# Moving the sums for block products and the mixer's norm broadcast in a two-block network

## The chip, the cores and the metric

The kernel runs on one core of a Trainium2 chip. The metric is the device time of one execution in microseconds (us). The median of three runs before the change is 1705.44 (1704.96 to 1706.16). Engines: TensorE (PE, matmuls), VectorE (DVE), ScalarE (ACT), GpSimd (POOL), SyncE (SP, issues DMAs).

## The reference

The input x has 512 tokens of 1024 features, in float32. A first block of two layers (gated linear attention beside differential attention) is followed by a second block, cut here to what matters:

```python
def swiglu(h, w_in, w_out):
    gate, up = jnp.split(h @ w_in, 2, axis=-1)
    return (jax.nn.silu(gate) * up) @ w_out

def hybrid_mixer(h, w_in, ...):
    za, zb, zg = jnp.split(h @ w_in, [2 * A_WIDTH, 2 * A_WIDTH + 3 * B_WIDTH], axis=-1)
    u, v = jnp.split(jax.nn.gelu(za), 2, axis=-1)
    y_a = spatial_gating(u, v, sgu_norm, sgu_w, sgu_b) @ w_proj_a   # v is normed in it
    ...
    return merged @ w_out

x = x + 0.5 * swiglu(rmsnorm(x, ffn1_norm), ffn1_w_in, ffn1_w_out)
x = x + hybrid_mixer(rmsnorm(x, mix_norm), ...)
x = x + 0.5 * swiglu(rmsnorm(x, ffn2_norm), ffn2_w_in, ffn2_w_out)
return rmsnorm(x, final_norm)
```

## The kernel before

x stays on the chip as eight tiles `xs[k]` of 128 features x 512 tokens. Each float32 product is three fp32r matmuls (`mm3`, L174 to L176): both operands are split into a rounded part hi (ACT copies it) and a rest lo (DVE subtracts). So every tile of weights costs ACT and DVE work before PE can use it.

Large products are done as 2x2 block products with seven multiplications instead of eight (`block_jobs`, L367). A unit loads four raw weight tiles of 1 MB (a11, a21, a22, a12), and forms sums of them: one by an adding DMA on POOL's queue (L393), a21 + a22 (L399) and a21 - a11 (L405) on DVE, one more by an adding DMA (L409). `parts` (L376) splits such a sum into hi and lo; for a name in `turn`, lo is made by a negated ACT copy and an adding POOL DMA (L383, L384) instead of DVE. Seven steps of 24 matmuls follow, in three accumulators (tm): step 0 uses x itself (xgh, xgl), steps 1 and 2 use sums of x (bth, btl), step 3 other sums (bnh, bnl). A `hook` is called after each half step; in steps 0, 2 and 3 it copies an accumulator out of PSUM (fa at L1083 in the feed-forward, va at L1243 in the mixer), and only then can the next step write there.

The sums of x are made by `block_sums(p)` (L323 to L342) for each of four pairs of x tiles: ACT makes te, bth and bnh, DVE the sums tt and te (L330 to L333), btl (L165) and bnl (L340). `t4_parts` (L345) later splits another part of te into xg.

The feed-forward starts with two ordinary input jobs of two products each (`in_job`, hidden tiles fg, fu, fh), then come units of block products. In the first feed-forward each of these four products is followed by one block sum. The mixer starts with the unit v; three of its block sums are made as x is finished (`after`, L301), the fourth from the hook at the start of step 0. `norm` makes the roots of the mean square: narrow matmuls nps (L245), a power on POOL (rs, L229), and 2 us of estimated time later a broadcast by eight matmuls nbc (L256) and the copy rsb (L259).

What sets the order: the jobs are generators. `run` (L186) issues them along an estimated clock and puts in side work (`light`, such as `norm` with its two delays) once it is due; behind that, a scheduler with an estimated timeline sets each engine's final row. Each engine executes its row strictly in order, so an instruction that waits holds all that stands behind it.

Of the kernel before, what the change touches and what calls it, by code (L numbers as in the profile page):

```python
# [13 lines left out]
ALU = mybir.AluOpType  # L14
# [53 lines left out]
PAUSE = 5.0  # L68
TURN = 10.0
TURN0 = 1.5  # L70


@with_exitstack
def block_kernel(ctx: ExitStack, tc: tile.TileContext, a, out):
# [219 lines left out]
                k0 += 1  # L294
                yield 2.6 * n / S

    def residual(o, k, scale, nxt, sums=False):

        V.scalar_tensor_tensor(xs[k], o, scale, xs[k], op0=ALU.mult, op1=ALU.add)
        after(k, nxt, sums)  # L300

    def after(k, nxt, sums=False):
        if k == 0:
            for key in ("rs", "bc", "nrs", "nrs2"):
                st.pop(key, None)
            st["xg"], st["bt"], st["bn"], st["be"] = [], [], [], []
        sumsq(k)
        st["xg"].append(split(xs[k], "xg", scale=nxt(k)))
        if sums and k in (2, 4, 6):
            block_sums(k // 2 - 1, nxt)  # L310
        if k == KT - 1:
            light(norm(2.5, 2.0))

# [48 lines left out]
        A.activation(hi, x, AF.Copy, scale=g)  # L364
        V.scalar_tensor_tensor(lo, x, g, f(hi), op0=ALU.mult, op1=ALU.subtract)

    def block_jobs(src, hook, turn=()):  # L367


        q, banks = {}, {}  # L370

        def load(name, i):
            q[name] = wraw.tile([P, 2112], F32, tag="raw", name=nm("raw"))[:, 0:4 * S]
            nc.sync.dma_start(q[name], src[i])

        def parts(name):  # L376
            pieces = []
            for j in range(2):
                r = q[name][:, 2 * j * S:2 * j * S + 2 * S]
                hi, lo = (wsp.tile([P, 1024], F32R, tag=v, name=nm(v)) for v in ("hi", "lo"))  # L380
                A.activation(hi, r, AF.Copy)  # L381
                if name in turn:
                    A.activation(lo, r, AF.Copy, scale=-1.0)  # L383
                    nc.gpsimd.dma_start(lo, r, accum_op=ALU.add)  # L384
                else:
                    V.tensor_tensor(lo, r, f(hi), op=ALU.subtract)  # L386
                pieces.append(tuple(v.rearrange("p (k n) -> p k n", n=S) for v in (hi, lo)))
            return pieces

        def l1():  # L390
            load("a11", 0)
            load("a21", 2)
            nc.gpsimd.dma_start(q["a21"], q["a11"], accum_op=ALU.add)  # L393
            return parts("a11")

        def l2():
            load("a22", 3)
            ps = parts("a21")
            V.tensor_tensor(q["a21"], q["a21"], q["a22"], op=ALU.add)  # L399
            return ps  # L400

        def l3():
            load("a12", 1)
            ps = parts("a21")
            V.tensor_tensor(q["a11"], q["a21"], q["a11"], op=ALU.subtract)  # L405
            return ps

        def l4():
            nc.gpsimd.dma_start(q["a21"], q["a12"], accum_op=ALU.add)  # L409
            return parts("a11")  # L410


        steps = [
            (l1, "b11", "a", True), (l2, "t3", "b", True), (l3, "t2", "a", False), (l4, "t1", "a", False),
            (lambda: parts("a12"), "b21", "c", True), (lambda: parts("a22"), "t4", "b", False),
            (lambda: parts("a21"), "b22", "a", False),
        ]

        def step(i, name, chain, first):
            def body(ps):  # L420
                if first:
                    banks[chain] = [psum("tm") for _ in range(2)]
                hook(i, -1, banks)
                for t in range(2):
                    for p in range(4):
                        ah, al = block(name, p, t)
                        wh, wl = (v[:, p % 2] for v in ps[p // 2])
                        mm3(banks[chain][t], ah, al, wh, wl, first and p == 0, p == 3, True)
                        yield 0.68
                    hook(i, t, banks)  # L430
            return body

        return [(ld, None, step(i, *which)) for i, (ld, *which) in enumerate(steps)]


# [601 lines left out]
    def ffn_jobs(i, nxt):  # L1037
# [3 lines left out]
        def in_job(c):  # L1041
            def body(ps):
                xg = st["xg"]
                os = []
                for j in range(2):
                    o = psum("fm")
                    yield from fm1(o, [ps[j]], xg)
                    os.append(o)

                    if i == 0:  # L1050
                        block_sums(2 * c + j, gains)
                    elif c + j == 0:
                        block_sums(3, gains)
                yield from until("bc")
                g = slot("fg")
                V.tensor_tensor(g, os[0], st["bc"], op=ALU.mult)
                A.activation(g, g, AF.Silu)
                u = slot("fu")
                V.tensor_tensor(u, os[1], st["bc"], op=ALU.mult)
                V.tensor_tensor(g, g, u, op=ALU.mult)  # L1060
                hid.append(split(g, "fh"))
            return body
# [12 lines left out]
        def unit(n):  # L1075
            v, h = {}, {"more": n not in (0, 2, 4)}

            def hook(i, t, banks):
                if t < 0:
                    return  # L1080
                if i in (0, 2, 3):
                    v[i, t] = slot("fa")
                    A.activation(v[i, t], banks["a"][t], AF.Copy)  # L1083
                if i == 1 and n == 0 and t == 1:
                    for p in range(4):
                        t4_parts(p)
                if i == 3:
                    V.tensor_tensor(v[3, t], v[3, t], banks["b"][t], op=ALU.add)
                if i == 4:
                    V.tensor_tensor(v[0, t], v[0, t], banks["c"][t], op=ALU.add)  # L1090
                    A.activation(v[0, t], v[0, t], AF.Silu, scale=roots("rs", t))
                if i == 5:
                    V.tensor_tensor(v[2, t], v[2, t], banks["b"][t], op=ALU.add)
                    V.scalar_tensor_tensor(v[0, t], v[2, t], roots("nrs", t), v[0, t], op0=ALU.mult, op1=ALU.mult)
                    h[t] = v[0, t]
                if i == 6:
                    g = slot("fg")
                    A.activation(g, banks["a"][t], AF.Silu, scale=roots("rs", 2 + t))
                    V.scalar_tensor_tensor(g, v[3, t], roots("nrs", 2 + t), g, op0=ALU.mult, op1=ALU.mult)
                    h[2 + t] = g  # L1100
                    if t == 1:
                        light(turned(h), TURN if h["more"] else TURN0)

            return block_jobs(a[f"ffs{i}"][n], hook)

        def add_out(o, k, hf):
            if hf < 2:
                V.scalar_tensor_tensor(xs[k], o, 0.5, xs[k], op0=ALU.mult, op1=ALU.add)
            elif nxt is not None:
                residual(o, k, 0.5, nxt, True)  # L1110
            else:
                V.scalar_tensor_tensor(xs[k], o, 0.5, xs[k], op0=ALU.mult, op1=ALU.add)
                sumsq(k)
                gain(k)
# [94 lines left out]
    def mixer_jobs():  # L1209
# [16 lines left out]
        def v_unit():  # L1226
# [7 lines left out]
                gv[t, b] = g, ss  # L1234

            def hook(i, t, banks):
                if t < 0:
                    if i == 0:
                        block_sums(3, gains)
                    return  # L1240
                if i in (0, 2, 3):
                    v[i] = v.get(i, []) + [slot("va")]
                    A.activation(v[i][t], banks["a"][t], AF.Copy)  # L1243
# [17 lines left out]
                            A.activation(g, g, AF.Copy, scale=r)  # L1261
                        vs.append((g0, g1))

            return block_jobs(a["mv"], hook, ("a11",))

        def conv(n, h):

# [12 lines left out]
        def cx_unit(n):  # L1280
            v, h = {}, {}

            def hook(i, t, banks):
                if t < 0:
                    return
                if i in (0, 2, 3):
                    v[i, t] = slot("ca")
                    A.activation(v[i, t], banks["a"][t], AF.Copy)
                for at, chain, k in ((3, "b", 3), (4, "c", 0), (5, "b", 2)):
                    if i == at:  # L1290
                        V.tensor_tensor(v[k, t], v[k, t], banks[chain][t], op=ALU.add)
                if i == 5:
                    V.scalar_tensor_tensor(v[0, t], v[2, t], roots("nrs2", t), v[0, t], op0=ALU.mult, op1=ALU.mult)
                    h[t] = v[0, t]
                    if t == 1 and n == 1:
                        for p in range(4):
                            block_b12(p, gains)
                if i == 6:
                    V.scalar_tensor_tensor(v[3, t], v[3, t], roots("nrs2", 2 + t), banks["a"][t], op0=ALU.mult, op1=ALU.mult)
                    h[2 + t] = v[3, t]  # L1300
                    if t == 1:
                        light(conv(n, h), TURN)
# [192 lines left out]
```

## Time and profile before

| | |
|---|---|
| median of three runs | 1705.44 us |
| profiled execution | 1705.94 us |
| its span in the trace | 1704.1 us |
| PE busy | 1653.0 us, 97% |
| DVE busy | 1131.6 us, 66% |
| ACT busy | 811.5 us, 48% |
| POOL busy | 119.2 us, 7% |

The span runs from the first to the last instruction; 1.84 us of the profiled execution lie outside it. A share of busy time is an average over the whole program; what one place costs is read from the timeline there. A row of a timeline gives the start, the duration, the engine, the line, the operation and the operands without buffer numbers, and in brackets the idle time just before it with what ended it.

### The profile page before, as it was taken

The numbers are of one execution on the slowest core, as the hardware profiler recorded it, in microseconds if no ns is written. First come the engines' busy times: TensorE is split into PE (matmuls) and PEld (weight loads), VectorE is DVE, ScalarE is ACT, GpSimd is POOL, SyncE is SP. The second block draws the span as 40 slices with busy tenths as digits, with TensorE's granted clock in tenths as the row PEclk, the third lists the DMA queues.
The fourth block names the chain that finished last, engine by engine and source line by source line (L and its number), as shares of the span: only waits on it lengthen the run. The fifth ranks groups of instructions, "written<-read, shape, count | busy, mean of one in ns | idle before, by whom it ended". The sixth has DMA issues, their size and how long they took to land.

```text
span 1704.1 us, 20537 instructions
## 1 busy us (share of the span) xinstructions
PE 1653.0 (97%) x8080; PEld 1366.5 (80%) x8080; DVE 1131.6 (66%) x1673; ACT 811.5 (48%) x1347; POOL 119.2 (7%) x104
## 2 busy tenths in 40 slices
PE   6898999999999999999998999999999999999998
PEld 5786778797888778888887888888888888888887
DVE  8788867958765856764766787534544765764754
ACT  4566554447564543543556654322323553552543
POOL 3020000420010000000002100000000000000000
PEclk9999999999999999999999999999999999999999
DMA  8534423421213153553553654222222334561531
GB/s 313 197 126 147 158 91 124 174 99 50 75 50 108 47 162 104 167 155 101 148 172 75 186 162 152 94 99 99 97 90 94 109 99 130 148 187 61 155 93 50
DMA packets 32449, 210.79 MB, mean 124 GB/s; under 512 B 3648, under 2 KB 3808, under 8 KB 8928
## 3 DMA queue, kind: packets, MB, share of 16 engines
q1 hardware_dynamic: 28032, 180.11, 29.5%
q0 software_dynamic: 4320, 29.36, 8.9%
q8 instruction: 63, 1.03, 0.2%
q14 instruction: 34, 0.28, 0.0%
HBM read 178.00 MB, written 2.10 MB: 106 GB/s over the span
## 4 chain that ended last, share of the span: by engine, by line
PE 84%; DVE 7%; ACT 4%; DMA 3%; issue 1%; POOL 1%; SPq 0%; DVEq 0%; POOLq 0%; ACTq 0%
PE fm L174 15%; PE fm L175 15%; PE fm L176 15%; PE tm L174 12%; PE tm L175 11%; PE tm L176 11%; DMA ada<-in_ada 2%; DVE ada L448 1%; DVE lo L150 1%; PE ht L1071 1%; PE sc L811 1%; DVE cv L574 1%; PE o L847 1%; PE sg L1314 0%; ACT hi L149 0%
## 5 line engine op out<-in xcount | busy, mean ns | idle before, releaser
L149 ACT ACTIVATE hi<-raw 128x1024 fp32r<-128x1024 f32 (+2 forms) x184 | 188.0, 1025 | 338.8 <-PE fm L175 272.1
L386 DVE TENSOR_TENSOR lo<-raw,hi 128x1024 fp32r<-128x1024 f32 x178 | 215.9, 1223 | 107.7 <-ACT hi L381 106.4
L381 ACT ACTIVATE hi<-raw 128x1024 fp32r<-128x1024 f32 x182 | 191.4, 1057 | 175.6 <-PE tm L176 85.3
L150 DVE TENSOR_TENSOR lo<-raw,hi 128x1024 fp32r<-128x1024 f32 (+2 forms) x184 | 217.4, 1183 | 43.4 <-ACT hi L149 39.7
L174 PE MATMUL tm<-hi,xgh 128*128 128x512 f32 x480 | 179.7, 395 | 12.0 <-ACT hi L615 12.0
L175 PE MATMUL tm<-lo,xgh 128*128 128x512 f32 x480 | 187.9, 394 | 0.2 <-DVE lo L616 0.2
L176 PE MATMUL tm<-hi,xgl 128*128 128x512 f32 x480 | 185.4, 393 | 0.0
L174 PE MATMUL fm<-fhh,hi 128*128 128x512 f32 (+1 forms) x368 | 140.0, 383 | 0.0
L175 PE MATMUL fm<-fhl,hi 128*128 128x512 f32 (+1 forms) x368 | 139.9, 380 | 0.0
L176 PE MATMUL fm<-fhh,lo 128*128 128x512 f32 (+1 forms) x368 | 139.9, 380 | 0.0
L174 PE MATMUL fm<-xgh,hi 128*128 128x512 f32 x320 | 125.8, 393 | 0.0
L175 PE MATMUL fm<-xgl,hi 128*128 128x512 f32 x320 | 124.5, 390 | 0.0
L176 PE MATMUL fm<-xgh,lo 128*128 128x512 f32 x320 | 124.4, 390 | 0.0
L174 PEld LDWEIGHTS tm<-hi,xgh 128*128 128x128 f32 x480 | 91.3, 191 | 31.3 <-ACT hi L615 12.4
L174 PE MATMUL fm<-hh,hi 128*128 128x512 f32 x256 | 106.7, 419 | 1.7 <-DVE cv L574 1.7
L175 PEld LDWEIGHTS tm<-lo,xgh 128*128 128x128 f32 x480 | 91.4, 190 | 19.8 <-DVE lo L616 0.7
L176 PEld LDWEIGHTS tm<-hi,xgl 128*128 128x128 f32 x480 | 91.2, 190 | 19.0
L175 PE MATMUL fm<-hl,hi 128*128 128x512 f32 x256 | 101.5, 396 | 0.0
L176 PE MATMUL fm<-hh,lo 128*128 128x512 f32 x256 | 101.3, 396 | 0.0
L174 PE MATMUL tm<-hi,bth 128*128 128x512 f32 x208 | 80.8, 402 | 8.3 <-ACT va L1243 4.2
L176 PE MATMUL tm<-hi,btl 128*128 128x512 f32 x208 | 80.7, 397 | 0.8 <-DVE btl L165 0.8
L175 PE MATMUL tm<-lo,bth 128*128 128x512 f32 x208 | 81.3, 399 | 0.0
(310 smaller groups left out, 3437.5 us busy)
## 6 DMA issues: line engine op xcount, KB each, us to landing
raw<-in_ffs SPq DMA_DIRECT2D x40, 1024.0 KB, 5.0
raw<-raw POOLq DMA_DIRECT2D x26, 1024.0 KB, 8.0
ada<-in_ada SPq DMA_DIRECT2D x23, 1024.0 KB, 4.8
raw<-in_wfm SPq DMA_DIRECT2D x16, 1024.0 KB, 4.8
raw<-in_ffo SPq DMA_DIRECT2D x16, 1024.0 KB, 5.0
raw<-in_mgp SPq DMA_DIRECT2D x16, 1024.0 KB, 4.8
raw<-in_wo SPq DMA_DIRECT2D x8, 1024.0 KB, 4.8
raw<-in_mcx SPq DMA_DIRECT2D x8, 1024.0 KB, 6.3
```

What stands on the lines that cost most here:

```text
L149: A.activation(hi, src_p, AF.Copy)
L150: V.tensor_tensor(lo, src_p, f(hi), op=ALU.subtract)
L174: T.matmul(o, wh, ah, start=start, stop=False, skip_group_check=open)
L175: T.matmul(o, wh, al, start=False, stop=False, skip_group_check=open)
L176: T.matmul(o, wl, ah, start=False, stop=stop, skip_group_check=open)
L381: A.activation(hi, r, AF.Copy)
L386: V.tensor_tensor(lo, r, f(hi), op=ALU.subtract)
L448: V.scalar_tensor_tensor(w, w, 1.0, cact, op0=ALU.mult, op1=ALU.mult, accum_out=t)
L574: V.scalar_tensor_tensor(c[:, sh:S], ps[:, 0:S - sh], tap[3 - sh], c[:, sh:S], op0=ALU.mult, op1=ALU.add)
L811: T.matmul(pss[m][:, 0:n], qk[hd][0][p][r, i * P:(i + 1) * P], qk[hd][1][q_][r, 0:n], start=p + q_ == 0, stop=False)
L847: T.matmul(on[hd][:, i * P:(i + 1) * P], et[:, j * P:(j + 1) * P], vt[j][:, hd * P:(hd + 1) * P], start=j == 0, stop=j == i)
L1071: T.transpose(ps[:, t * P:(t + 1) * P], h[t][:, c * P:(c + 1) * P], ident)
```

## The change

Four edits. The sums of x come earlier: in the first feed-forward two pairs after each of the first two products, and for the mixer the last pair right behind the last tile of x (also for the second feed-forward). The two weight sums on DVE are issued from the body of steps 0 and 1, after their first half, and no longer while the weights are split. The norm's broadcast before the mixer is due 12 us after the roots on the estimated clock instead of 2. And only l1's a11 is split by ACT and POOL in the mixer's unit v; l4's is split by DVE.

```diff
-    def after(k, nxt, sums=False):
+    def after(k, nxt, sums, rest):
...
         if k == KT - 1:
-            light(norm(2.5, 2.0))
+            light(norm(2.5, rest))
+            if sums:
+                block_sums(k // 2, nxt)
...
-                if name in turn:
+                if turn:
...
-            return parts("a11")
+            return parts("a11", turn)
         def l2():
             load("a22", 3)
-            ps = parts("a21")
-            V.tensor_tensor(q["a21"], q["a21"], q["a22"], op=ALU.add)
-            return ps
+            return parts("a21")
         def l3():
             load("a12", 1)
-            ps = parts("a21")
-            V.tensor_tensor(q["a11"], q["a21"], q["a11"], op=ALU.subtract)
-            return ps
+            return parts("a21")
+        def sums(i):
+            if i == 0:
+                V.tensor_tensor(q["a21"], q["a21"], q["a22"], op=ALU.add)
+            if i == 1:
+                V.tensor_tensor(q["a11"], q["a21"], q["a11"], op=ALU.subtract)
...
-                hook(i, -1, banks)
...
                     hook(i, t, banks)
+                    if t == 0:
+                        sums(i)
...
-                    if i == 0:
-                        block_sums(2 * c + j, gains)
-                    elif c + j == 0:
-                        block_sums(3, gains)
+                    if i == 0 and c == 0:
+                        for p in (2 * j, 2 * j + 1):
+                            block_sums(p, gains)
...
-                residual(o, k, 0.5, nxt, True)
+                residual(o, k, 0.5, nxt, True, REST)
...
-                if t < 0:
-                    if i == 0:
-                        block_sums(3, gains)
-                    return
...
-            return block_jobs(a["mv"], hook, ("a11",))
+            return block_jobs(a["mv"], hook, True)
```

The engines' rows differ in two places only: at the start of the first feed-forward's unit, and in the mixer's unit v. Numbers behind a name tell buffers apart, and differ between the two programs; a line's number is up to some ten higher in the new program.

PE at the start of the mixer's unit v, before. nps ends step 0's stretch; tm_1755 is the accumulator of step 2, tm_1776 that of step 1:

```order
L175 MATMUL tm_1755_8212<-lo_1775_8288,bth_1742_8160 128x512
L176 MATMUL tm_1755_8212<-hi_1774_8287,btl_1743_8161 128x512
L174 MATMUL tm_1755_8212<-hi_1774_8287,bth_1760_8223 128x512
L175 MATMUL tm_1755_8212<-lo_1775_8288,bth_1760_8223 128x512
L256 MATMUL nbc_1768_8268<-identr_82,rh_1766_8255 128x128
L174 MATMUL tm_1776_8292<-hi_1751_8203,bth_1704_7984 128x512
L175 MATMUL tm_1776_8292<-lo_1752_8204,bth_1704_7984 128x512
L176 MATMUL tm_1776_8292<-hi_1751_8203,btl_1705_7985 128x512
```

After; tm_1774 and tm_1775 are those of step 1, tm_1760 that of step 2, bth_1753 the sum of the last pair of x:

```order
L175 MATMUL tm_1775_8281<-hi_1758_8222,bth_1742_8160 128x512
L176 MATMUL tm_1775_8281<-lo_1759_8223,bth_1742_8160 128x512
L177 MATMUL tm_1775_8281<-hi_1758_8222,btl_1743_8161 128x512
L175 MATMUL tm_1774_8280<-hi_1758_8222,bth_1753_8210 128x512
L176 MATMUL tm_1774_8280<-lo_1759_8223,bth_1753_8210 128x512
L175 MATMUL tm_1775_8281<-hi_1758_8222,bth_1753_8210 128x512
L176 MATMUL tm_1775_8281<-lo_1759_8223,bth_1753_8210 128x512
L175 MATMUL tm_1760_8226<-hi_1770_8272,bth_1704_7984 128x512
L176 MATMUL tm_1760_8226<-lo_1771_8273,bth_1704_7984 128x512
```

Step 1 now stands ahead of step 2, and the matmuls on the last pair of x stand at the end of it.

ACT at the same place, before; va_1762 empties the accumulator for step 2, bth_1760 is the sum of the last pair:

```order
L329 ACTIVATE te_1757_8214<-x6_113,cols_76 128x512
L381 ACTIVATE hi_1772_8283<-raw_1730_8105 128x1024
L381 ACTIVATE hi_1774_8287<-raw_1730_8105 128x1024
L164 ACTIVATE bth_1760_8223<-tt_1758_8215 128x512
L1243 ACTIVATE va_1762_8241<-tm_1755_8212 128x512
```

After:

```order
L332 ACTIVATE te_1750_8201<-x6_113,cols_76 128x512
L384 ACTIVATE hi_1770_8272<-raw_1730_8105 128x1024
L384 ACTIVATE hi_1772_8276<-raw_1730_8105 128x1024
L384 ACTIVATE hi_1776_8316<-raw_1729_8103 128x1024
L165 ACTIVATE bth_1753_8210<-tt_1751_8202 128x512
L1243 ACTIVATE va_1762_8240<-tm_1760_8226 128x512
L1243 ACTIVATE va_1768_8268<-tm_1761_8227 128x512
```

hi_1776, the first half of the weights of step 3, has come between the hi of step 2 and bth.

DVE at the start of the first feed-forward's unit, before; lo_1343 is the first operand that step 2 needs, fg_1328 the second job's hidden tile:

```order
L399 TENSOR_TENSOR raw_1309_5756<-raw_1309_5756,raw_1332_5859 128x2048
L330 SCALAR_TENSOR_TENSOR tt_1324_5835<-x6_113,cols_76,te_1323_5834 128x256
L405 TENSOR_TENSOR raw_1308_5754<-raw_1309_5756,raw_1308_5754 128x2048
L331 SCALAR_TENSOR_TENSOR tt_1324_5835<-tt_1324_5835,te_1323_5834 128x256
L386 TENSOR_TENSOR lo_1343_5903<-raw_1309_5756,hi_1342_5902 128x1024
L386 TENSOR_TENSOR lo_1345_5907<-raw_1309_5756,hi_1344_5906 128x1024
L332 TENSOR_TENSOR te_1323_5834<-te_1323_5834 128x256
L165 TENSOR_TENSOR btl_1327_5844<-tt_1324_5835,bth_1326_5843 128x512
L1056 TENSOR_TENSOR fg_1328_5849<-fm_1314_5767,rsb_1298_5709 128x512
L1059 TENSOR_TENSOR fu_1329_5852<-fm_1322_5809,rsb_1298_5709 128x512
L386 TENSOR_TENSOR lo_1349_5947<-raw_1308_5754,hi_1348_5946 128x1024
L333 SCALAR_TENSOR_TENSOR te_1323_5834<-x6_113,ng_1325_5836,tt_1324_5835 128x256
```

After:

```order
L1066 TENSOR_TENSOR fg_1316_5776<-fg_1316_5776,fu_1317_5779 128x512
L351 TENSOR_TENSOR xgl_1273_5592<-te_1311_5761,xgh_1272_5591 128x256
L389 TENSOR_TENSOR lo_1336_5866<-raw_1321_5788,hi_1335_5865 128x1024
L166 TENSOR_TENSOR fhl_1319_5783<-fg_1316_5776,fhh_1318_5782 128x512
L1062 TENSOR_TENSOR fg_1328_5849<-fm_1326_5799,rsb_1303_5724 128x512
L1065 TENSOR_TENSOR fu_1329_5852<-fm_1327_5824,rsb_1303_5724 128x512
L410 TENSOR_TENSOR raw_1321_5788<-raw_1321_5788,raw_1332_5859 128x2048
L1066 TENSOR_TENSOR fg_1328_5849<-fg_1328_5849,fu_1329_5852 128x512
L412 TENSOR_TENSOR raw_1320_5786<-raw_1321_5788,raw_1320_5786 128x2048
L389 TENSOR_TENSOR lo_1343_5903<-raw_1321_5788,hi_1342_5902 128x1024
L389 TENSOR_TENSOR lo_1345_5907<-raw_1321_5788,hi_1344_5906 128x1024
L166 TENSOR_TENSOR fhl_1331_5856<-fg_1328_5849,fhh_1330_5855 128x512
```

The sums of x (L330 to L340) have gone from here to an earlier place, and the weight sums (L410, L412) stand behind the first hidden tile.

## Rows read from the trace of the kernel before

**Rows 1.** PE's waits of the whole span: line waited for, us in total, times, longest us.

```profile
PE tm L174 <- ACT va L1243: 4.2, 1, 4.2
PE tm L174 <- ACT fa L1083: 4.1, 1, 4.1
```

**Rows 2.** Windows: the granted clock is the figure behind the five engines' busy times.

```profile
598.10:602.60 4.50, 4.44 (x11) 3.48 (x12) 0.93 (x2) 0.49 (x2) 0.00 (x0) 0.50 0.69 204
606.00:880.00 274.00, 274.00 (x1249) 227.41 (x1249) 171.02 (x178) 121.84 (x150) 7.71 (x9) 1.00 0.49 144
919.40:923.40 4.00, 3.94 (x9) 3.14 (x10) 3.07 (x9) 0.62 (x3) 2.90 (x2) 0.50 0.16 33
```

**Rows 3.** Timeline of PE, first feed-forward: start, us, what, idle before and releaser.

```profile
581.98 0.39 PE L174 MATMUL tm<-hi,xgh 128*128 128x512 f32 x1
...
587.42 0.39 PE L174 MATMUL tm<-hi,bth 128*128 128x512 f32 x1
...
593.34 0.73 PE L176 MATMUL tm<-hi,btl 128*128 128x512 f32 x2 [0.77 <-DVE btl L165]
...
598.16 0.80 PE L174 MATMUL tm<-hi,bth 128*128 128x512 f32 x1 [4.08 <-ACT fa L1083]
...
605.84 0.39 PE L174 MATMUL tm<-hi,bnh 128*128 128x512 f32 x1
```

**Rows 4.** Timeline of ACT, first feed-forward.

```profile
574.86 1.28 ACT L1057 ACT_TABLE_LOAD   x1
...
596.99 0.63 ACT L164 ACTIVATE fhh<-fg 128x512 fp32r<-128x512 f32 x1 [0.43 <-DVE fg L1060]
...
597.52 1.07 ACT L1083 ACTIVATE fa<-tm 128x512 f32<-128x512 f32 x2
```

**Rows 5.** Timeline of DVE, first feed-forward.

```profile
577.76 1.23 DVE L386 TENSOR_TENSOR lo<-raw,hi 128x1024 fp32r<-128x1024 f32 x1 [0.25 <-ACT hi L381]
...
584.53 0.42 DVE L348 TENSOR_TENSOR xgl<-te,xgh 128x256 fp32r<-128x256 f32 x1
...
584.87 2.29 DVE L399 TENSOR_TENSOR raw<-raw,raw 128x2048 f32<-128x2048 f32 x1
...
587.07 0.48 DVE L330 SCALAR_TENSOR_TENSOR tt<-x,cols,te 128x256 f32<-128x256 f32 x1
...
592.61 0.68 DVE L165 TENSOR_TENSOR btl<-tt,bth 128x512 fp32r<-128x512 f32 x1
```

**Rows 6.** Timeline of PE, mixer.

```profile
914.28 0.94 PE L245 MATMUL nps<-ones,sq 128*128 128x1 f32 x8
...
919.46 0.79 PE L174 MATMUL tm<-hi,bth 128*128 128x512 f32 x1 [4.24 <-ACT va L1243]
...
934.88 0.50 PE L175 MATMUL tm<-lo,bnh 128*128 128x512 f32 x1 [0.97 <-DMA lo<-raw]
...
961.98 0.39 PE L174 MATMUL tm<-hi,bth 128*128 128x512 f32 x1
```

**Rows 7.** Timeline of ACT, mixer.

```profile
914.69 2.00 ACT L381 ACTIVATE hi<-raw 128x1024 fp32r<-128x1024 f32 x2 [2.37 <-DVE raw L399]
...
918.30 0.63 ACT L164 ACTIVATE bth<-tt 128x512 fp32r<-128x512 f32 x1 [1.60 <-DVE tt L331]
...
918.83 0.58 ACT L1243 ACTIVATE va<-tm 128x512 f32<-128x512 f32 x1
```

**Rows 8.** Timeline of POOL, first feed-forward and mixer.

```profile
564.55 1.14 POOL L229 TENSOR_TENSOR rs<-rin,mhalf 128x4 f32<-128x4 f32 x1 [18.83 <-DVE rin L228]
...
915.88 5.55 POOL L229 TENSOR_TENSOR rs<-rin,mhalf 128x4 f32<-128x4 f32 x1 [14.79 <-DVE rin L228]
...
960.61 2.59 POOL L229 TENSOR_TENSOR mr<-rin,mhalf 128x1 f32<-128x1 f32 x1 [1.22 <-DVE rin L228]
```

**Rows 9.** Timeline of DVE, mixer.

```profile
915.65 2.28 DVE L405 TENSOR_TENSOR raw<-raw,raw 128x2048 f32<-128x2048 f32 x1
...
918.18 2.35 DVE L386 TENSOR_TENSOR lo<-raw,hi 128x1024 fp32r<-128x1024 f32 x2
```

More of the change, by code (lines that the diff above doesn't have):

```diff
@@ L70 @@
 TURN0 = 1.5
+REST = 12.0
 @with_exitstack
@@ L295, in tm, with residual @@
                 yield 2.6 * n / S
-    def residual(o, k, scale, nxt, sums=False):
+    def residual(o, k, scale, nxt, sums=False, rest=2.0):
         V.scalar_tensor_tensor(xs[k], o, scale, xs[k], op0=ALU.mult, op1=ALU.add)
-        after(k, nxt, sums)
-    def after(k, nxt, sums=False):
+        after(k, nxt, sums, rest)
+    def after(k, nxt, sums, rest):
         if k == 0:
@@ L365, in block_b12, with block_jobs @@
         V.scalar_tensor_tensor(lo, x, g, f(hi), op0=ALU.mult, op1=ALU.subtract)
-    def block_jobs(src, hook, turn=()):
+    def block_jobs(src, hook, turn=False):
         q, banks = {}, {}
@@ L374, in load, with parts @@
             nc.sync.dma_start(q[name], src[i])
-        def parts(name):
+        def parts(name, turn=False):
             pieces = []
@@ L1236, in hook @@
             def hook(i, t, banks):
-                if t < 0:
-                    if i == 0:
-                        block_sums(3, gains)
-                    return
                 if i in (0, 2, 3):
@@ L1283, in hook @@
             def hook(i, t, banks):
-                if t < 0:
-                    return
                 if i in (0, 2, 3):
```

## The prediction

> **What bounds the kernel now.** I read the shares of busy time first: TensorE (PE) is busy 97% of the span, so a change that moves no matmul away can only win what PE loses in waits or at a lower clock. The second view is PE's waits by what ended them. Two of the larger ones lie in the part that the change touches: 4.1 us for ScalarE (ACT)'s copy fa at L1083 (the start of the first feed-forward) and 4.2 us for its copy va at L1243 (the start of the mixer) [rows 1]. Third, the granted clock by windows: it is 0.50 right after each of these two waits, and 1.00 in a 274 us stretch without a wait [rows 2]; of the engine's two levels, 1.2 and 2.4 GHz, that is the lower one and the upper one. Fourth, the timelines of these two places.
>
> *Place A, first feed-forward* [rows 3]. Step 0 of the first block product starts at 581.98 and step 1 at 587.42: 24 matmuls in 5.44, so 0.2267 us each at the upper clock. Steps 1 and 2, 48 matmuls, should take 10.88, but the first matmul of step 3 (bnh) starts at 605.84: 18.42. The excess of 7.54 is the 0.77 wait for btl, the 4.08 wait for fa, and then matmuls at half the clock. Why is fa late? ACT takes it at 597.52, straight behind fhh, which waited for VectorE (DVE)'s product fg [rows 4]. DVE is the cause: until 598 it works without a gap on sums of x (L330 to L340), sums of weights (L399, L405: 2.29 and 2.28), btl and lo [rows 5].
>
> *Place B, mixer* [rows 6]. After step 0 and the eight narrow nps matmuls (0.94), PE stands still for 4.24 and resumes at 919.46. In order, eleven matmuls of step 2 (tm_1755) stand ahead of all of step 1 (tm_1776), so step 1 waits with them for va, and va stands in ACT's row behind hi and bth, which wait for DVE: hi for the sum L399, bth for tt, which is queued behind L405 (915.65, 2.28) [rows 7, 9]. From nps at 914.28 to step 1 of the next unit at 961.98 are 47.70 us; its 168 matmuls (144 of steps 1 to 6, 24 of the next step 0) at 0.2267 are 38.09, with nps and the eight of nbc at 0.94 each 39.97. Excess 7.73, of it 0.97 a wait for the DMA that makes lo out of raw at 934.88.
>
> **The change part by part.**
>
> *A: sums of x pulled forward, sums of weights put behind.* Four block sums are issued during the first two products instead of all four products; work is moved, none is added. In the new order DVE has, from the lo at 577.76 on, 19 instructions up to the lo that step 2 needs first (lo_1343): three lo (a pair takes 2.35 [rows 9], so 1.17 each: 3.5), six of 256 columns (0.34 each: 584.53 to 584.87 [rows 5], one scalar_tensor_tensor at 0.40: 2.1), eight of 512 columns (0.68 less the 0.08 by which starts overlap: 4.8) and the two weight sums (584.87 to 587.07, 2.20 each: 4.4). The sum is 14.8, so lo_1343 is ready at 592.5. ACT's table load (1.28 [rows 4]) moves behind the sums, in front of the last hi that DVE waits for: I add 0.3, 592.8. PE reaches that operand 26 matmuls after 587.42, at 593.3. Slack 0.5. The first product's fg and fhh stand before the weight sums, so fa is free of them. So neither btl nor fa nor lo should hold PE; no pause, no fall of the clock. Bounds: gain 7.5 if all is hidden; if DVE is 2 us later than I add up, PE pauses 1.5 and gains 6.0; if it is over 4 late, a pause like today's returns with its slow matmuls, gain near 2. I take 7.4.
>
> *B: block_sums(3) right behind the last tile of x; weight sums in the body of steps 0 and 1; the broadcast later.* The last pair of x was summed from a hook of step 0 already, so DVE's load stays, and its tt remains behind L412 (L405 before, over at 915.65 + 2.20 = 917.85). What changes is PE's row: 15 matmuls of step 1 that need no late operand, then three more, come straight after nps, 915.22 to 919.30. The 19th needs bth_1753, and on ACT a new hi (hi_1776, for l4) stands ahead of it: it is freed by the 15th matmul at 918.8, takes 1.0 (a pair takes 2.00 [rows 7]), and bth follows till 920.4 (0.63). So PE waits 1.2 where it waited 4.24. Does the clock fall for that? After the wait of 0.97 at 934.88 the matmul's own row is 0.50, after the two long waits 0.79 and 0.80 [rows 3, 6]: the short pause left the upper clock, so I take no. Then va (0.58) is ready at 921.0, four matmuls later at 921.4 it is needed. rs comes from GpSimd (POOL) at 921.4 (915.88 and 5.55 [rows 8]); its broadcast nbc now is first needed at 923.9. Before, nbc stood between the slow matmuls and cost no wait of its own, so REST itself is worth nothing but order: between 0 and 0.5, I take 0.
>
> *B: l4's lo by DVE instead of ACT and a POOL DMA.* Two ACT copies and two DMAs go, two DVE subtractions of 1.17 come. Step 3 needs them 30 matmuls and nbc after 920.5, at 928.2; DVE has the first behind bth's tt and the two lo that end at 920.5, near 922, the second near 927.6 for a use at 930, as its hi is freed by the 17th matmul from 921.4, at 925.3. So the matmuls of steps 1 and 2 hide them; without that cover they would cost their 2.3. The wait of 0.97 goes. The raw tile that the DMAs held is freed sooner, so the next unit's load on SP's queue and POOL's adding DMA, both queued for that tile, start sooner; l1 keeps its two DMAs, so nothing waits longer on POOL's queue. Gain 0.97, between 0 and 1.0.
>
> Sum for B: excess 7.73 less 1.2 for bth, less 0.1 for small steps of the hi ring: 6.4. At the end of the unit DVE makes the next unit's weight sums while POOL makes the last root mr (960.61, 2.59 [rows 8]); this comes 6.4 earlier, but in a like order. I take 0.2 off: 6.2. Bounds for B: 7.7, and 2 if the pause for bth grows to 4 and takes the clock down with it.
>
> The third place that the code touches, the second feed-forward, has the same row on every engine.
>
> Profiled execution: 1705.94, span 1704.1 and 1.84 outside. 1705.94 - 7.4 - 6.2 = 1692.3; it lies 0.50 above the median 1705.44 of the runs, so 1691.8 for the median.
>
> The Trainium skill ("TensorE: Matmul & The Clock Gate", section "Wait — 56ns, not 53.3ns?") gives 426.7 ns from start to start for 512 columns at the lower clock and 215.7 at the upper. The trace's slow matmuls (598.16 and on) lie near the first; its fast ones, 0.2267, do not reach the second. By the page's figure the two excesses would be 8.1 and 9.6 and the new time near 1689.5; stretches without waits run at 0.2267 too, so the measurement decides.
>
> **The rivals.**
>
> R1, DVE is late in A. For it: a slack of 0.5 us behind 14.8 us of summed rows is thin, and each POOL instruction or late hi eats it. Against: before, DVE did the same work with the products' sums in the middle. Price 1 to 5.5, I take 4 (half of today's loss): 1695.8.
>
> R2, POOL's root blocked by DVE. The root rs took 1.14 at 564.55 and 5.55 at 915.88, where DVE ran two-input sums back to back [rows 8, 9]. At the end of unit v the last mr root meets the next unit's two sums of 2.2 (moved behind its first matmuls); four va scalings and then ca and hi, which PE needs, queue on ACT behind it. Price: nothing to 4.4 (5.55 less 1.14), I take 3: 1694.8. It decides if mr takes over 3 us. The Trainium skill ("SBUF — State Buffer", section "Who interferes with whom") says that a DVE instruction with both inputs in SBUF and a GpSimd instruction that reads SBUF exclude each other for a whole instruction; the two durations of rs agree with it.
>
> R3, the change does not do what it says: the estimated order looks better but ACT's row keeps PE waiting (bth behind hi_1776, fa behind hi), the pauses return elsewhere. For it: the order is made on estimated times. Against: each wait in the new rows can be replayed with durations of before. Time near 1704 to 1706.
>
> R4, slower. One mechanism: the granted clock. If PE without its pauses were granted less over the long stretch behind, 606 to 880, 274 us at 0.95 would cost 274 x (1/0.95 - 1) = 14.4, above the whole gain; it decides from about 0.95 on, and at 0.94 (17.5) the time is 1709. Against it: that stretch has no wait now and shows 1.00 [rows 2].
>
> **How the numbers follow.** Forecast 0.75 (own range 1690.2 to 1693.5), R1 0.09, R2 0.08, R3 0.04, R4 0.04. The upper end goes to the prices taken for R1 and R2, 1696.5; the lower to both excesses gone whole (1705.44 - 7.54 - 7.73 = 1690.2), less 0.4 for spread. Less than 0.2% (3.4 us) can't be told from no change: faster 0.92 (forecast, R1, R2), same 0.04, slower 0.04.
>
> **What would show it.** Right: PE's waits no longer list fa L1083 with 4 us, va L1243 drops from the list, a wait for bth of about 1.2 appears near 919, and windows at 598 and 920 show a clock of 1.00; step 3 of A starts near 598.3, step 1 of the next unit near 955.6. Wrong: a wait for lo_1343 near 593 (R1); a root mr of 3 us or more and a wait of PE for hi or ca behind it (R2); new waits of 4 us with half the clock (R3); under 1.00 between 600 and 880 (R4).

## The result and the profile after

The changed kernel takes 1691.71 us in the median of three runs against 1705.20 for the kernel before, a ratio of 0.9921 (95% interval 0.9901 to 0.994), 13.5 us less. The prediction was 1691.8. A fourth run, the profiled one, had a granted clock of 0.75 from end to end and took 2060.35 us, so it is left out here (with it the median is 1692.21) and the rows below are of a repeat of the changed kernel. The repeat has a profiled execution of 1690.06 us with a span of 1687.9, and five runs with a median of 1690.97 against 1703.64 beside them, ratio 0.9919 (0.9907 to 0.9932).

Lines are those of the new program. Place A starts 2.8 us earlier here than in the trace of before (584.65 against 587.42); such differences ahead of it come and go between executions (592.03 in one run below). From place A's end to place B's start the two traces agree within 0.5 us (308.44 and 307.99), and behind place B within 0.3, so no third place has a part in the gain.

PE at place A, start and duration first:

```profile
584.65 0.39 PE L175 MATMUL tm<-hi,bth 128*128 128x512 f32 x1
...
590.09 0.61 PE L175 MATMUL tm<-hi,bth 128*128 128x512 f32 x2
590.55 0.39 PE L176 MATMUL tm<-lo,bth 128*128 128x512 f32 x1
...
595.53 0.61 PE L175 MATMUL tm<-hi,xgh 128*128 128x512 f32 x2
...
595.99 0.39 PE L175 MATMUL tm<-hi,bnh 128*128 128x512 f32 x1
```

Step 1 starts at 584.65, step 2 at 590.09, step 3 at 595.99. Against [rows 3] nothing waits between step 1 and step 3: 11.34 us instead of 18.42. It is 0.46 over the 10.88 of 48 matmuls, since two matmuls of a later step (595.53) now stand ahead of step 3. The waits for btl and fa are gone, so the place gained 7.1 us from step 1 to step 3, and 7.5 if those two matmuls are taken off.

DVE and then ACT at the same place:

```profile
574.84 1.23 DVE L389 TENSOR_TENSOR lo<-raw,hi 128x1024 fp32r<-128x1024 f32 x1 [0.26 <-ACT hi L384]
...
583.97 2.29 DVE L410 TENSOR_TENSOR raw<-raw,raw 128x2048 f32<-128x2048 f32 x1
586.17 0.69 DVE L1066 TENSOR_TENSOR fg<-fg,fu 128x512 f32<-128x512 f32 x1
586.77 2.29 DVE L412 TENSOR_TENSOR raw<-raw,raw 128x2048 f32<-128x2048 f32 x1
588.97 2.36 DVE L389 TENSOR_TENSOR lo<-raw,hi 128x1024 fp32r<-128x1024 f32 x2
```

```profile
577.81 1.28 ACT L1063 ACT_TABLE_LOAD   x1
...
586.35 2.01 ACT L384 ACTIVATE hi<-raw 128x1024 fp32r<-128x1024 f32 x2 [2.22 <-DVE raw L410]
588.27 0.61 ACT L165 ACTIVATE fhh<-fg 128x512 fp32r<-128x512 f32 x1
588.78 1.06 ACT L1087 ACTIVATE fa<-tm 128x512 f32<-128x512 f32 x2
```

These answer to [rows 4, 5]. DVE is still busy almost without a pause, but what PE needs now stands first: lo_1343 is the first of the two at 588.97 and, at 1.23 for one, ready at 590.20. PE uses it 26 matmuls after 584.65, at 590.55. fa starts 4.1 us after PE's step 1 (588.78 against 584.65), where it was 10.1 in [rows 3, 4]. The two fa are over at 589.84, and the first two matmuls of step 2, which need one each, start at 590.09.

PE at place B, and ACT there:

```profile
903.98 0.95 PE L246 MATMUL nps<-ones,sq 128*128 128x1 f32 x8
...
910.16 0.50 PE L175 MATMUL tm<-hi,bth 128*128 128x512 f32 x1 [0.99 <-ACT bth L165]
910.49 0.40 PE L176 MATMUL tm<-lo,bth 128*128 128x512 f32 x1
...
945.53 0.62 PE L175 MATMUL tm<-hi,bth 128*128 128x512 f32 x2
```

```profile
904.39 2.01 ACT L384 ACTIVATE hi<-raw 128x1024 fp32r<-128x1024 f32 x2 [2.37 <-DVE raw L410]
908.53 1.06 ACT L384 ACTIVATE hi<-raw 128x1024 fp32r<-128x1024 f32 x1 [2.12 <-PE tm L177]
909.49 0.61 ACT L165 ACTIVATE bth<-tt 128x512 fp32r<-128x512 f32 x1
910.01 1.06 ACT L1243 ACTIVATE va<-tm 128x512 f32<-128x512 f32 x2
```

From nps to the next unit's step 1 are 41.55 us instead of the 47.70 of [rows 6]. The next unit's step 1 is the row at 945.53. One wait is left, 0.99 for bth, which stands behind the hi at 908.53 as its row foretold; va, which held PE in [rows 7], no longer does. The granted clock by windows (the figure behind five pairs of busy times), and the roots on POOL:

```profile
584.60:595.90 11.30, 11.30 (x51) 9.35 (x51) 10.83 (x9) 7.23 (x10) 0.93 (x1) 1.00 0.29 58
903.90:918.70 14.80, 13.81 (x68) 11.08 (x67) 11.74 (x20) 8.21 (x13) 6.42 (x2) 1.00 0.36 72
606.00:880.00 274.00, 274.00 (x1250) 227.35 (x1249) 175.24 (x184) 123.56 (x153) 7.70 (x9) 1.00 0.50 145
```

```profile
905.58 5.55 POOL L230 TENSOR_TENSOR rs<-rin,mhalf 128x4 f32<-128x4 f32 x1 [14.78 <-DVE rin L229]
...
939.49 4.14 POOL L230 TENSOR_TENSOR mr<-rin,mhalf 128x1 f32<-128x1 f32 x4 [13.91 <-DVE rin L229]
```

The clock is at its upper level in all three, where two of the windows of [rows 2] showed 0.50. rs takes its 5.55 again [rows 8], hidden; the four mr roots take 4.14 together, the longest of them 1.49, and PE waits for nothing behind them.

### The profile page after: what moved, and what is told of

It reads as the page before. It is cut to its first block, busy times and chain, and to the rows that moved or that the text cites. A ratio compares the mean times of both kernels' runs of the same rounds, so it can differ in the third digit from the quotient of the medians.

```text
span 2058.2 us, 20532 instructions
## 1 busy us (share of the span) xinstructions
PE 2028.4 (99%) x8080; PEld 1465.0 (71%) x8080; DVE 1140.8 (55%) x1675; ACT 815.4 (40%) x1345; POOL 111.7 (5%) x102
## 4 chain that ended last, share of the span: by engine, by line
PE 96%; ACT 1%; DVE 1%; DMA 0%; POOL 0%; issue 0%; SPq 0%; POOLq 0%; DVEq 0%; ACTq 0%
PE fm L175 17%; PE fm L176 17%; PE fm L177 17%; PE tm L176 13%; PE tm L175 13%; PE tm L177 12%; PE ht L1077 1%; PE sc L818 1%; PE o L854 1%; PE at L845 0%; PE go L971 0%; PE sg L1312 0%; PE ot L520 0%; PE qt L803 0%; DMA x<-in_xT 0%; PE u L949 0%
## 5 line engine op out<-in xcount | busy, mean ns | idle before, releaser
L175 PE MATMUL tm<-hi,xgh 128*128 128x512 f32 x480 | 209.2, 459 | 11.4 <-ACT hi L622 11.4
L176 PE MATMUL tm<-lo,xgh 128*128 128x512 f32 x480 | 220.1, 461 | 0.1
L177 PE MATMUL tm<-hi,xgl 128*128 128x512 f32 x480 | 217.3, 459 | 0.0
L175 PE MATMUL fm<-fhh,hi 128*128 128x512 f32 (+1 forms) x368 | 163.9, 448 | 0.0
L176 PE MATMUL fm<-fhl,hi 128*128 128x512 f32 (+1 forms) x368 | 163.6, 445 | 0.0
L177 PE MATMUL fm<-fhh,lo 128*128 128x512 f32 (+1 forms) x368 | 163.3, 444 | 0.0
L175 PE MATMUL fm<-xgh,hi 128*128 128x512 f32 x320 | 148.4, 464 | 0.0
L176 PE MATMUL fm<-xgl,hi 128*128 128x512 f32 x320 | 146.4, 458 | 0.0
L177 PE MATMUL fm<-xgh,lo 128*128 128x512 f32 x320 | 145.4, 455 | 0.0
L177 PEld LDWEIGHTS fm<-fhh,lo 128*128 128x128 f32 x368 | 73.6, 200 | 28.8
```

The costliest lines, as they stand in the source:

```text
L175: T.matmul(o, wh, ah, start=start, stop=False, skip_group_check=open)
L176: T.matmul(o, wh, al, start=False, stop=False, skip_group_check=open)
L177: T.matmul(o, wl, ah, start=False, stop=stop, skip_group_check=open)
```

## The experiments

"Place A" is the time from step 1 to step 3 there, "place B" the time from nps to the next unit's step 1, both on PE; the changed kernel has 11.34 and 41.55, the kernel before 18.42 and 47.70.

**The changed kernel again.** 

> The changed kernel once more, for its times and its trace. Theory of the prediction: about 1691.8 us, ratio 0.992; no wait for fa or for lo_1343 in the first feed-forward, step 3 there near 598.3; in the mixer a single wait of about 1.2 us for bth near 919 at a clock that stays at 1.00. Rivals: a wait near 593 (DVE late), a root mr over 3 us with a wait of PE behind it, or half the clock after the 1.2 us pause (about 2 us more).

Measured 1690.97. The first theory's waits and clock came as above, and none of the rivals' did. Step 3 of place A came at 595.99 instead of 598.3, which is the 2.8 us of the earlier start. The wait for bth came at 910.16 and not near 919: the place named left out the 7.4 us that are gained ahead of it.

**Early block sums undone.**

```diff
-                    if i == 0 and c == 0:
-                        for p in (2 * j, 2 * j + 1):
-                            block_sums(p, gains)
+                    if i == 0:
+                        block_sums(2 * c + j, gains)
```

> The changed kernel with one edit undone: in the first feed-forward each of the four products is followed by one block sum again. Theory of the prediction: all of place A's gain hangs on this edit, since DVE's row there is then the old one: 7.4 us slower than the changed kernel, about 1699.3, with the waits for btl (0.8) and fa (4.1) and half the clock behind them back. Rival: the weight sums, still issued in the bodies of the steps, carry part of it, and half or more of the 7.4 stays.

Measured 1698.36, ratio to before 0.9963 (0.995 to 0.9976), 7.4 slower than the changed kernel. Place A took 18.24, with the old waits (PE):

```profile
586.46 0.39 PE L175 MATMUL tm<-hi,bth 128*128 128x512 f32 x1
...
592.39 0.73 PE L177 MATMUL tm<-hi,btl 128*128 128x512 f32 x2 [0.78 <-DVE btl L166]
...
597.20 0.80 PE L175 MATMUL tm<-hi,bth 128*128 128x512 f32 x1 [4.08 <-ACT fa L1086]
...
604.70 0.39 PE L175 MATMUL tm<-hi,bnh 128*128 128x512 f32 x1
```

The weight sums were still issued from the bodies of the steps here, so the whole of A hangs on where the sums of x are issued.

**Early broadcast again.** REST is the delay of the mixer's broadcast behind the roots, 12.0 in the changed kernel. Edit: `REST = 2.0`. 

> The changed kernel with one edit undone: the mixer's broadcast is due 2 us after the roots again. The prediction took this edit to be worth 0 (0 to 0.5): 1691.8 to 1692.3. A new theory, from PE's row: with 2.0 the eleven matmuls of step 2 stand ahead of step 1 again, so the wait for va of about 4.2 us and half the clock behind it come back, and only the 0.97 us of the DMA wait stay won: 5.3 us slower than the changed kernel, about 1697.2.

Measured 1695.37 (0.9946, 0.9932 to 0.996), 4.4 slower; place B 45.93, again 4.4 more. PE's row there:

```profile
903.29 0.95 PE L246 MATMUL nps<-ones,sq 128*128 128x1 f32 x8
...
908.48 0.74 PE L175 MATMUL tm<-hi,bth 128*128 128x512 f32 x1 [4.25 <-ACT va L1243]
909.02 0.63 PE L176 MATMUL tm<-lo,bth 128*128 128x512 f32 x1
...
949.22 0.39 PE L175 MATMUL tm<-hi,bth 128*128 128x512 f32 x1
```

The wait for va is back (4.25 against 4.24 in [rows 6]), and so is the slow clock. The new theory holds: the delay of the broadcast, not the place of the last block sum, puts step 1 ahead of step 2.

**l4's lo from ACT and POOL again.**

```diff
             nc.gpsimd.dma_start(q["a21"], q["a12"], accum_op=ALU.add)
-            return parts("a11")
+            return parts("a11", turn)
```

> The changed kernel with one edit undone: l4's lo in the unit v comes from a negated ACT copy and an adding POOL DMA again. One of the two copies then stands ahead of bth on ACT. Theory: bth is 1.0 us later, PE waits 2.2 instead of 1.2, and the DMA is in time as its copy is 9 us earlier than before: 1.0 us slower than the changed kernel, about 1692.8. Rival: the wait for the DMA of about 1.0 returns beside it, or the longer pause takes the clock down: 2 to 4 us slower.

Measured 1696.25 (0.9952, 0.9939 to 0.9964), 5.3 slower, not 1.0; place B 47.43. The theory missed, and its rival was too small too. On PE, and on POOL:

```profile
904.91 0.95 PE L246 MATMUL nps<-ones,sq 128*128 128x1 f32 x8
...
912.04 0.50 PE L175 MATMUL tm<-hi,bth 128*128 128x512 f32 x1 [1.93 <-ACT bth L165]
...
925.72 0.80 PE L176 MATMUL tm<-lo,bnh 128*128 128x512 f32 x1 [3.59 <-DMA lo<-raw]
926.32 0.63 PE L177 MATMUL tm<-hi,bnl 128*128 128x512 f32 x1
...
952.34 0.39 PE L175 MATMUL tm<-hi,bth 128*128 128x512 f32 x1
```

```profile
912.04 0.90 POOL L387 DMA_DIRECT2D lo<-raw  x1
912.65 1.19 POOL L415 DMA_DIRECT2D raw<-raw  x1
914.63 0.86 POOL L387 DMA_DIRECT2D lo<-raw  x1 [0.79 <-ACT xgh L350]
```

The wait for bth grew from 0.99 to 1.93, by the 1.0 that was expected. But the second lo, issued at 914.63, holds PE until 925.72, and the clock falls behind it. A 1 MB adding DMA stands between the two lo on POOL's queue.

**The early block sums alone, on the kernel before.** 

> The kernel before with the first feed-forward's block sums pulled forward (and the weight sums issued from the bodies of the steps), the mixer as before: last block sum from the hook, broadcast due after 2 us, both a11 by ACT and POOL. Theory: place A as in the changed kernel (11.3 us from step 1 to step 3), place B as before (47.7 us from nps to the next unit's step 1, with the waits for va 4.2 and for the DMA 1.0): 7.1 us faster than the kernel before. Rival: the places are coupled by the DMA queues, and B moves by more than 0.5 us either way.

Measured 1696.54 against 1705.06, ratio 0.9951 (0.9935 to 0.9967): 8.5 us faster, and the interval holds the 7.1. Place A 11.33, place B 47.44 with its old waits of 4.25 and 0.97: the places are not coupled.

**The later broadcast alone, on the kernel before.** The line that counts (the others pass the new argument on):

```diff
-                residual(o, k, 0.5, nxt, True)
+                residual(o, k, 0.5, nxt, True, 12.0)
```

> The kernel before with the later broadcast alone (12 instead of 2 on the estimated clock). PE's row in the mixer is then that of the changed kernel (step 1 ahead of step 2), but l4's lo still comes from ACT and a POOL DMA. Theory, that this edit and the one on l4's lo pay only together: place B takes 47.4 us as with l4's edit undone (waits: about 1.9 for bth, 3.6 for the DMA, half the clock behind it), so 0.3 us faster than the kernel before. Rival, that the edits add up: the 4.4 us that this edit was worth in the changed kernel, 4.4 us faster.

Measured 1705.97 against 1705.06: ratio 1.0004 (0.9995 to 1.0013), no gain. Place B took 48.60, with these waits:

```profile
919.11 0.50 PE L174 MATMUL tm<-hi,bth 128*128 128x512 f32 x1 [1.94 <-ACT bth L164]
...
932.79 0.79 PE L175 MATMUL tm<-lo,bnh 128*128 128x512 f32 x1 [3.62 <-DMA lo<-raw]
```

The wait for va was turned into one for a DMA. Place B is 1.2 over the 47.4 expected, as PE's matmuls ran slow for 5.4 us behind that wait and for 2.9 in the run with l4's edit undone. The two edits do not add up; they pay together.

**The two other edits undone.** The last block sum from the hook, the weight sums while the weights are split. The main lines; the same is done in `l3`, and the second feed-forward's first product is followed by its last block sum:

```diff
-            if sums:
-                block_sums(k // 2, nxt)
...
             load("a22", 3)
-            return parts("a21")
+            ps = parts("a21")
+            V.tensor_tensor(q["a21"], q["a21"], q["a22"], op=ALU.add)
+            return ps
...
-                    if t == 0:
-                        sums(i)
...
-            return block_jobs(a["mv"], hook, True)
+            return block_jobs(a["mv"], hook, True, lambda: block_sums(3, gains))
```

> The changed kernel with two edits undone: the last block sum comes from the hook of step 0 (and from the second feed-forward's first product), and the weight sums are issued while the weights are split. The built rows of all engines are the same as those of the changed kernel, so theory: no difference, 12.7 us faster than the kernel before. Rival: none by the rows; a difference over 1.5 us would say that repeated runs of one program differ by that much.

Measured 1691.93 against 1705.06 (0.9919, 0.9905 to 0.9933); place A 11.33, place B 41.50. The one wait of PE in place B is the changed kernel's:

```profile
910.52 0.50 PE L175 MATMUL tm<-hi,bth 128*128 128x512 f32 x1 [0.99 <-ACT bth L165]
```

The engines' rows are the same as with both edits, so these two parts of the change are together worth nothing.

**DVE 2.2 us later at place A.** `more` is 1 in the first unit of the first feed-forward and 0 elsewhere:

```diff
+                for _ in range(more):
+                    V.tensor_tensor(q["a21"], q["a21"], q["a21"], op=ALU.max)
                 V.tensor_tensor(q["a21"], q["a21"], q["a22"], op=ALU.add)
```

> The changed kernel with one more DVE instruction of 128x2048 (2.2 us, the maximum of a weight tile with itself) ahead of the first weight sum of the first feed-forward's first unit. A small product (0.6) also moves ahead of lo_1343 in DVE's row. Theory: DVE's chain is the limit of place A with a slack of 0.4 us, so lo_1343 is 2.8 us later and PE waits 2.4: 2.4 us slower than the changed kernel if the clock stays up, about 4.4 if it falls (it stayed up behind a wait of 1.9 and fell behind one of 3.6). Rival: DVE has more slack than the replay says, less than 1 us slower.

Measured 1694.78 against 1705.06 (0.9946, 0.9928 to 0.9964), 2.9 over the 1691.93 of the run above, which has the changed kernel's rows and was timed beside the same runs of the kernel before. Place A took 15.59 in the profiled execution, 4.25 more. On PE:

```profile
592.03 0.39 PE L175 MATMUL tm<-hi,bth 128*128 128x512 f32 x1
...
600.43 0.80 PE L176 MATMUL tm<-lo,bth 128*128 128x512 f32 x1 [2.11 <-DVE lo L389]
601.03 0.63 PE L177 MATMUL tm<-hi,btl 128*128 128x512 f32 x1
...
607.62 0.39 PE L175 MATMUL tm<-hi,bnh 128*128 128x512 f32 x1
```

The wait is 2.11, the clock falls behind it, and that doubles the price in this execution. It was the slowest of six (1701.38), with most of its excess ahead of place A; whether the clock falls here in the others, whose median is 2.9 over, is not shown. DVE's lo was 2.8 us later and PE waited 2.11 for it, so the slack behind DVE's row is under a microsecond, as replayed.

**l4's lo from ACT and POOL, without the 1 MB adding DMA.**

```diff
-            nc.gpsimd.dma_start(q["a21"], q["a12"], accum_op=ALU.add)
-            return parts("a11")
+            if turn:
+                V.tensor_tensor(q["a21"], q["a21"], q["a12"], op=ALU.add)
+            else:
+                nc.gpsimd.dma_start(q["a21"], q["a12"], accum_op=ALU.add)
+            return parts("a11", turn)
```

> The kernel with l4's edit undone (l4's lo from ACT and POOL DMAs), and the 1 MB adding DMA that stood between the two DMAs of lo on POOL's queue replaced by a DVE sum (128x2048, 2.2 us) in the unit v. With l4's edit undone the second of these DMAs was issued at 914.63 and PE waited for it till 925.72. Theory: the 1 MB transfer in between makes it late; without it it lands some 5 us after its issue (as where PE waited for it at 934.88 in the kernel before, issued at 930.33), about 920 against a need at 922, so the wait of 3.6 and the half clock behind it go, and only the 1.9 for bth stays: place B about 42.5 us instead of 47.4, 4.3 us faster than with l4's edit undone, near 1692. Rival: DMAs of lo take 11 us here anyway, and the wait stays at 2 us or more.

Measured 1691.96 against 1704.19 (0.9921, 0.9908 to 0.9935): the wait for the DMA is gone. Place B took 43.75, 1.2 more than expected, since the same wait for bth let the clock fall this time:

```profile
912.92 0.68 PE L175 MATMUL tm<-hi,bth 128*128 128x512 f32 x1 [1.94 <-ACT bth L165]
913.40 0.63 PE L176 MATMUL tm<-lo,bth 128*128 128x512 f32 x1
...
923.02 0.40 PE L176 MATMUL tm<-lo,bnh 128*128 128x512 f32 x1
```

```profile
916.27 0.86 POOL L387 DMA_DIRECT2D lo<-raw  x1 [2.45 <-ACT lo L386]
```

The second lo, issued at 916.27, landed 6.2 us later instead of 11.1. So the transfer queued in between made the lo late, not the lo's own transfer. It landed 0.6 before PE read it (923.02); with the clock up, PE would have been there some 1.2 sooner, so a wait of about 0.6 could have been left.

**A smaller delay of the broadcast.** Edit: `REST = 5.0`. 

> The changed kernel with REST at 5.0 instead of 12.0. PE's row in the mixer has step 1 ahead of step 2 here too, with bth_1753 first needed after 18 matmuls, and some of the next steps' matmuls stand ahead of step 3. Theory: the size of REST matters only in that it flips the row: place B at 41.5 us within 0.5, no difference from the changed kernel. Rival: the broadcast 7 us earlier on the estimated clock costs a wait for its operands of 1 us or more.

Measured 1693.85 against 1704.19 (0.9933, 0.992 to 0.9946); place B 42.31, with a new wait of 0.53 for a lo:

```profile
919.64 0.49 PE L176 MATMUL tm<-lo,xgh 128*128 128x512 f32 x1 [0.53 <-DVE lo L389]
```

The flip of the row is the larger part by far (45.93 with 2.0), but the theory that nothing else depends on the size missed by 0.8 us. Whether the medians of this kernel and of the changed one differ is open: their intervals overlap.

## Why the prediction was right

The time, the two places and their sizes were right: A was put at 7.4 and measured 7.1 to 7.5, B at 6.2 and measured 6.15. What ended last was named in advance: the wait for bth came at 0.99 (1.2 predicted), behind the ACT instruction foretold, and the clock stayed up behind it. Of the signs, the times of place B were named from the old trace less B's own gain: with A's 7.4 taken off as well, step 1 of the next unit, put near 955.6, belongs near 948, and the trace, 2.8 us earlier from before A, has it at 945.53.

*DVE's row in A.* Its sum of 14.8, with 0.3 for the table load, was 15.4 in the trace (574.84 to 590.20), and the slack of 0.5 was 0.35. Rival R1 was right in what it feared, a thin slack, and not in its happening: one more DVE sum costs 2.9 us by the medians.

*fa in A.* The prediction wrote that "fa is free of" the weight sums, as the first product's fg and fhh stand before them. In the trace it is not: on ACT, fa stands behind two hi that waited 2.22 for the weight sum L410 (586.35), and behind the second job's fhh, whose fg (586.17) stands behind that sum on DVE. It was in time with 0.25 to spare (589.84 against 590.09), so this part of A's gain came out as forecast, but by luck and not for the reason given.

*The step that failed is the split of B among its edits.* The prediction wrote "REST itself is worth nothing but order: between 0 and 0.5, I take 0", and gave the new row to three edits under one heading. Undone together, the last block sum and the weight sums cost nothing; REST undone alone costs 4.4, as it flips the row. The prediction had the rows of the two kernels only, where all edits act at once.

*l4's lo* was priced at the wait that it removes, 0.97. With the old row it is worth 1.5 (47.44 to 45.93). With the new row PE reaches step 3 earlier, and the old way costs 5.9 (47.43 to 41.55), as the DMA is then too late. These are differences of single traces. The sum was right because both terms were read off the final rows: the error lay in the names on them.

Place B, nps to the next unit's step 1, in us:

| | broadcast early | broadcast late |
|---|---|---|
| l4's lo by ACT and POOL | 47.70, 47.44 | 47.43, 48.60 |
| l4's lo by DVE | 45.93 | 41.55, 41.50 |

*R2* did not come: PE waits for nothing behind the mr roots, none of which took over 1.49. rs took its 5.55 again in the changed kernel, while DVE ran back to back from 905.34 to 910.24; here the root was simply needed later. The Trainium skill ("SBUF — State Buffer", section "Who interferes with whom") says that a DVE instruction with two inputs in SBUF contends with a GpSimd instruction that reads SBUF; the 5.55 agrees with it. *R3* fails by the time, *R4* by the clock of 1.00 between 606 and 880.

## What to carry to other kernels

Read the final rows of every engine, with one edit at a time taken out, before crediting an edit: here the new places of the weight sums and of the mixer's last block sum leave all rows as they are, and an edit whose text only delays side work put 22 matmuls of step 1 ahead of a stalled group. An edit that removes a wait makes the next producer due earlier, so price its companions at the new due time: here the later broadcast alone gained nothing, since a DMA queued behind another one became the last to arrive. And a short wait of the matmul engine can cost twice its length when the clock falls behind it (4.25 us for a wait of 2.11).

## What the runs showed of the hardware

At the two places, the granted clock behind a wait of PE either stayed at 1.00 or fell to half, and the matmuls then ran slow for 2.9 to 5.4 us. It stayed up behind waits of 0.97, 0.99, 1.93 and one of 1.94; it fell behind another of 1.94, and behind 2.11, 3.59, 3.62, 4.08, 4.24 and 4.25. The 1.93 and the second 1.94 came at the same place of two programs that differ in one sum alone (l4's lo from ACT and POOL, with and without the 1 MB adding DMA). Elsewhere in the kernel before a wait of 1.88, over at 328.64, was followed by a clock of 0.50 from 329.6 to 336.4. So the length of the wait alone does not settle it; what does stays open.

An adding DMA of 512 KB on POOL's queue landed 4.5 us after its issue at 930.33 in the kernel before, and 11.1 us after its issue at 914.63 with l4's edit undone, where a 1 MB one had been issued 2 us ahead of it. That one took 10.5 us there, and 7.0 in the kernel before (issued at 921.40). Whether the queue's order or the shared transfer made the small one late was not separated.
